# A hybrid decoder layer on one core: an attention weight load issued earlier, 1/rms multiplications paired, output weight pieces split later

## The chip, the cores and the metric

The kernel runs on one core of a Trainium2 chip. Its time is the device time of one execution, in microseconds (us). The engines are named as in the profile: PE (TensorE, matrix products; PEld is its loading of weights), DVE (VectorE), ACT (ScalarE), POOL (GpSimd) and SP (SyncE, which here issues nearly all DMAs). Each engine works through its own instructions in order; an instruction waits on semaphores for what other engines or DMAs have to finish first.

## The reference

One decoder layer for 256 tokens of width 1024, in float32. `h` is the RMS-normed input; `q`, `k`, `v`, `u_pool` and the gate logits are five parts of one projection of it.

```python
h = rmsnorm(x, norm_mix_g)
proj = h @ w_in
q, k, v, u_pool, gate_logits = split(proj)
q, k = rotary(rmsnorm(heads(q), q_norm_g)), rotary(rmsnorm(heads(k), k_norm_g))
attn = moba_attention(q, k, heads(v))       # 256 tokens are one block: causal attention
pooled = multiscale_pool_mixer(u_pool, w_pool, pool_scale)
gates = sigmoid(gate_logits + b_gate)       # two gates, one for each branch
mixed = gates[0] * (attn @ w_branch_attn) + gates[1] * (pooled @ w_branch_pool)
x = x + mixed @ w_out
h2 = rmsnorm(x, norm_ffn_g)
gate, val = split(causal_depthwise_conv(h2 @ w_up, conv_w, conv_b))
return x + (silu(gate) * val) @ w_down
```

## The kernel before

**Three products for one.** Every matrix product is made of three matmuls in a reduced float format (`mm3`, lines 101 to 107): each operand is split into a high part, which is the rounded value, and a low part, which is the rest. The product is high times high, plus high times low, plus low times high. So every weight passes through three steps: a DMA of a chunk of 128 x 2048 floats (1 MB) into one of four raw buffers; ACT writes its high part (`high`, line 93), DVE its low part (`low`, line 97). Both work on pieces of half a chunk, 128 x 1024.

**The schedule of the pieces.** `order` (line 110) lists the chunks as they are used: q, k, v, the pooled input `p`, the gates `g`, `pool`, two chunks `bp` of the pooled branch, two chunks `ba` of the attention branch, four chunks `o` of the output projection, then the feed-forward network. A call of `ahead()` (line 201) emits at most one high half and one low half, the next in the list; the low halves follow one piece behind the high ones. `next_high` does nothing when the chunk is four or more ahead of the oldest one still in use (`WBUFS`, line 169). After the last low half of a chunk its raw buffer is free, and `loads()` (line 191) emits the next load. Where `ahead()` is called, then, fixes on ACT, DVE and SP what stands in front of what: the order of every engine is the order in which the code emits.

**The stretch around the change.** After sixteen gate tiles (`g0` to `g15`) come eight tiles of the pooled branch (`bp`, j = 0 to 7, loop of line 739), then eight of the attention branch (`ba`, loop of line 763), then the output projection. A tile is 128 features for all 256 tokens: 12 matmul steps for a branch tile, 24 for an output tile. The tiles of PSUM rotate over four banks.

In a tile of the pooled branch DVE evicts PSUM and multiplies with the gate, which ACT has put through the sigmoid (line 671). Six gate tiles (`PLAIN`) were evicted by ACT without the 1/rms factor, and DVE multiplies each by `R1` later (line 757). Ahead of pooled tile 5, TensorE multiplies the softmax weights with the values (line 640); DVE scales the result by the reciprocal sums `RS` (line 659), ACT and DVE split it into the high and the low part of `heads` (lines 660 and 664).

In a tile of the attention branch there is a chain: DVE multiplies PSUM with the gate (line 770), POOL adds the pooled branch's tile (line 771), ACT writes the high part `mh[j]` (line 772), DVE the low part `ml[j]` (line 774), which for j - 2 is emitted at tile j. `mh` and `ml` are the moving operands of the output projection: its first output tile goes over k = 0 to 6, then the second over k = 0 to 6, then both over k = 7 (line 820).

**Softmax weights.** The weights of a pair of heads are turned by way of DRAM: a write (`home_w`, line 298) and four reads back, called fills (`sm<-home_w`, line 306). The sums of the exponentials are inverted, turned and written too (`home_sums`, lines 603 to 606); one tick later `fill_late` emits eight fills and asks for one load, and another tick later `spread` asks for one more and reads the sums back to all partitions (`RS`, line 628). From gate tile 10 on ordinary loads are paused, so that only these emit any.

Of the kernel before, what the change touches and what calls it, by code (L numbers as in the profile page):

```python
# [10 lines left out]
ALU = mybir.AluOpType  # L11
# [44 lines left out]
MAPS = 6  # L56
VALUES = 4
LATE = 9
PIECES = (1, 1, 1, 1, 0, 1, 1, 1)
GATES = (4, 5, 0, 1, 2, 6, 7, 3)  # L60
PLAIN = (4, 5, 6, 7, 8, 9)
HALVED = 2
# [10 lines left out]
def hybrid_layer_kernel(ctx: ExitStack, tc: tile.TileContext, xq_d, xtok_d, par_d, wkv_d, wpg_d,  # L73
                        wpool_d, wba_d, wbp_d, wout_d, wup_d, wdn_d, out_d):
    nc = tc.nc
# [16 lines left out]
    def high(hi, src, scale=1.0):  # L92
        nc.scalar.activation(hi, src, AF.Copy, scale=scale)  # L93

    def low(lo, hi, src, scale=None):
        if scale is None:
            nc.vector.tensor_tensor(lo, src, hi.bitcast(F32), ALU.subtract)  # L97
        else:
            nc.vector.scalar_tensor_tensor(lo, src, scale, hi.bitcast(F32), ALU.mult, ALU.subtract)
# [25 lines left out]
    def load(parts=1):  # L125
        c = loaded[0]
        if c == len(order):
            return
        loaded[0] += 1
        name, src = order[c]  # L130
        n = src.shape[-1]
        if c in cut_loads:
            parts = 2
        raws[c] = raw_p.tile([P, CH], F32, tag="raw", name=f"raw_{name}{c}")
        for i in range(parts):
            sl = slice(i * n // parts, (i + 1) * n // parts)
            nc.sync.dma_start(out=raws[c][:, sl], in_=src[:, sl])
# [53 lines left out]
    def loads(most=None):  # L191

        while loaded[0] - RAWBUFS in split and order[loaded[0] - RAWBUFS][0] != "q" and loaded[0] < len(order):
            if paused[0] if most is None else most == 0:
                break
            load()
            most = most if most is None else most - 1
# [3 lines left out]
    def ahead(upto=0):  # L201

        next_high()
        next_low()
        if at[1] - sum(p[0] < used[0] for p in pieces) < upto:
            next_high()
            next_low()

    def chunk(name):
        c = used[0]  # L210
        used[0] += 1
        spent.update(i for i in range(c) if order[i][0] != "dn")
        assert order[c][0] == name and all(p[0] != c or name == "dn" and p[3] for p in pieces[at[1]:]), (name, order[c][0])
        return his[c], los[c]
# [63 lines left out]
    R1 = const.tile([P, S], F32, name="R1")  # L278
# [12 lines left out]
    def turn(y, x):  # L291

        blocks = "p (n b r) -> p n b r"
        nc.vector.transpose(y.rearrange("p (b n r) -> p n b r", b=4, r=32), x.rearrange(blocks, b=4, r=32))

    def spill(y, name):
        home = dram.tile([P, y.shape[-1]], F32, name=f"home_{name}")
        nc.sync.dma_start(out=home, in_=y)
        return home
# [134 lines left out]
    def later(n, fn, *args):  # L434
        due.setdefault(clock[0] + n, []).append((fn, args))

    def tick():
        clock[0] += 1
        for fn, args in due.pop(clock[0], []):
            fn(*args)  # L440
# [80 lines left out]
    def gate(n):  # L521
        return gates[:, n // 2, n % 2, :]
# [58 lines left out]
    def exponentials(hp, sm, mx, *flat):  # L581
        for j in range(2):
            for t in (1, 0):
                at = j * H + NT * hp + t
                nc.scalar.activation(sm[:, j, TOK[t]], sm[:, j, TOK[t]], AF.Exp, bias=mx[:, t, j:j + 1],
                                     scale=qs[:, t, 2 * hp + j:2 * hp + j + 1], accum_out=rsum[:, at:at + 1])
        if hp % 2:
            later(1, held.append, (turn_weights, hp, *flat))
        else:
            later(2, turn_weights, hp, *flat)  # L590
# [4 lines left out]
    def turn_weights(hp, y, sm):  # L595
        turn(y, sm)
        home = spill(y, f"w{hp}")
        if hp < 2:
            later(1 + hp, fill_weights, hp, home, sm)
            return  # L600
        late.append((hp, home, sm))
        if hp == H // 2 - 1:
            nc.vector.reciprocal(rsum[:, 0:2 * H], rsum[:, 0:2 * H])
            yr = const.tile([P, 32], F32, name="yr")
            nc.vector.transpose(yr, rsum)
            far = spill(yr, "sums")
            later(1, fill_late, far)

    late = []
# [22 lines left out]
    def values(hps):  # L632

        po = ps2.tile([P, 2, 512], F32, tag="ps2", name=f"ps_o{hps[0]}")
        for i, hp in enumerate(hps):
            for b in range(2):
                for j in range(2):
                    h = 2 * hp + j
                    out = po[j * DH:(j + 1) * DH, i, 0:S].rearrange("p (a t r) -> p a t r", a=4, r=32)
                    nc.tensor.matmul(out[:, :, b:2, :], vn[:, b, h * DH:(h + 1) * DH],  # L640
                                     soft[hp][:, :, 3 * j + 2 * b:3 * j + b + 2, :], start=b == 0, stop=b == 1)
        return po
# [10 lines left out]
    def rounded(hps, po):  # L653
        if not heads:
            both = act.tile([P, 2, KA, S], F32R, tag="at", name="heads")
            heads.extend(both[:, i] for i in range(2))
        for i, hp in enumerate(hps):
            v = weighed(hp)
            nc.vector.tensor_tensor(v, po[:, i, 0:S].rearrange("p (a t r) -> p a t r", a=4, r=32), v, ALU.mult)
            high(tokens(heads[0], hp), natural(hp))  # L660

    def rests(hps):
        for hp in hps:
            low(tokens(heads[1], hp), tokens(heads[0], hp), natural(hp))
# [3 lines left out]
    def sigmoids(n):  # L668
        for _ in range(min(n, len(waiting))):
            f = waiting.pop(0)  # L670
            nc.scalar.activation(gate(f), gate(f), AF.Sigmoid, bias=par[:, C_BG + f:C_BG + f + 1])
# [19 lines left out]
    plain = []  # L691
    for n in range(2 * KD):
# [26 lines left out]
        f = 2 * GATES[b] + c  # L719
# [11 lines left out]
    def branch(src, oph, opl, j, w):  # L731
        hi, lo = w
        ps = bank(f"ps_b{src}{j}")
        for k in range(4):
            sl = slice(k * 512 + (j % 4) * P, k * 512 + (j % 4 + 1) * P)
            mm3(ps[:, 0:S], (hi[:, sl], lo[:, sl]), (oph[:, k, :], opl[:, k, :]), k == 0, k == 3)
        return ps

    for j in range(KD):
        if j % 4 == 0:  # L740
            w = chunk("bp")
        ps = branch("p", poolh, pooll, j, w)
        if j == VALUES:
            pos = [(hps, values(hps)) for hps in ((0, 1), (2, 3))]
        if j in (VALUES, VALUES + 1):
            nc.vector.tensor_tensor(gate(KD + j), ps[:, 0:S], gate(KD + j), ALU.mult)
            for hps, po in pos:
                rounded(hps, po) if j == VALUES else rests(hps)
        if j % 2 == 1:
            tick()  # L750
        for _ in range(PIECES[j]):
            ahead()
        sigmoids(1)
        if j not in (VALUES, VALUES + 1):
            nc.vector.tensor_tensor(gate(KD + j), ps[:, 0:S], gate(KD + j), ALU.mult)
        if j < len(plain):
            nc.vector.tensor_tensor(gate(plain[j]), gate(plain[j]), R1, ALU.mult)
    mixer.close()
    tmp = ctx.enter_context(tc.tile_pool(name="ffn", bufs=2))
    mh = act.tile([P, KD, S], F32R, tag="qk", name="mh")  # L760
# [2 lines left out]
    for j in range(KD):  # L763
        if j % 4 == 0:
            w = chunk("ba")
        ps = branch("a", heads[0], heads[1], j, w)
        sigmoids(1)
        if j in (1, 3):
            ahead()
        nc.vector.tensor_tensor(gate(j), ps[:, 0:S], gate(j), ALU.mult)  # L770
        nc.gpsimd.tensor_tensor(gate(j), gate(j), gate(KD + j), ALU.add)
        high(mh[:, j, :], gate(j))
        if j > 1:
            low(ml[:, j - 2, :], mh[:, j - 2, :], gate(j - 2))
# [248 lines left out]
```

## Time and profile before

| what | value |
| --- | --- |
| time, median of 3 runs | 329.81 us (329.2 to 329.86) |
| the profiled execution's own time | 328.35 us |
| its span in the trace | 326.5 us |
| busy: PE / DVE / ACT / POOL | 322.2 / 260.4 / 201.9 / 71.9 us |
| HBM read, written | 65.61 MB, 3.69 MB |

The span runs from the first to the last instruction in the trace; the profiled execution's own time has 1.85 us more around it. Busy time is the sum of an engine's instructions, without those that only wait, branch or issue DMAs. A row of a timeline has the start, the duration, the engine, the line, the operation and what it writes and reads; in square brackets stands how long the engine had been idle before it, and what ended that. Where rows are merged (x2 and more) the duration is that of all.

### The profile page before, as it was taken

How to read it: one execution, taken by the hardware profiler on the slowest of the kernel's cores; microseconds unless marked ns; L12 is line 12 of the kernel's file. 1: busy time of each engine (PE TensorE's matmuls, PEld its weight loads, DVE VectorE, ACT ScalarE, POOL GpSimd, SP SyncE). 2: the span in 40 equal slices, each digit the busy share in tenths (PEclk: the TensorE clock that was granted, in tenths of full speed). 3: DMA queues.
4: the chain of work that ended last, by engine and by line, in shares of the span. 5: the costliest groups of instructions: out<-in, count | busy, mean ns of one | idle time of the engine just before them, and what ended most of it. 6: DMA issues, size and time to landing. Idle time of an engine off the chain costs nothing.

```text
span 326.5 us, 6772 instructions
## 1 busy us (share of the span) xinstructions
PE 322.2 (99%) x2708; PEld 315.7 (97%) x2708; DVE 260.4 (80%) x451; ACT 201.9 (62%) x329; POOL 71.9 (22%) x89
## 2 busy tenths in 40 slices
PE   8999999999999999999999999999999999999995
PEld 8888899999999999999999999999999999999995
DVE  5839989999988986869997978686868686868834
ACT  5767619575968657668675647464646464646520
POOL 1007690000000070230421221212121212121330
PEclk9999999999999999999999999999999999999999
DMA  7999799838789743635437546464646464643003
GB/s 264 421 418 234 223 358 305 296 135 287 262 267 320 310 168 131 257 131 202 186 113 275 196 192 229 161 236 153 223 165 225 164 226 162 223 165 130 0 2 129
DMA packets 16542, 69.72 MB, mean 214 GB/s; under 512 B 2176, under 2 KB 7040, under 8 KB 9856
## 3 DMA queue, kind: packets, MB, share of 16 engines
q1 hardware_dynamic: 16096, 69.17, 59.8%
q8 instruction: 21, 0.34, 0.4%
q10 hardware_dynamic: 416, 0.13, 0.3%
q14 instruction: 9, 0.07, 0.1%
HBM read 65.61 MB, written 3.69 MB: 212 GB/s over the span
## 4 chain that ended last, share of the span: by engine, by line
PE 99%; DVE 0%; issue 0%
PE ps_up L106 12%; PE ps_up L105 12%; PE ps_up L107 12%; PE ps_d L884 6%; PE ps_d L883 6%; PE ps_d L885 6%; PE ps_g L105 4%; PE ps_g L106 4%; PE ps_g L107 4%; PE ps_q L335 3%; PE ps_k L335 3%; PE ps_v L335 3%; PE ps_out L106 2%; PE ps_out L107 2%; PE ps_out L105 2%; PE ps_warm L250 1%
## 5 line engine op out<-in xcount | busy, mean ns | idle before, releaser
L107 PE MATMUL ps_up<-hhi,lo_up 128*128 128x256 f32 x352 | 97.2, 276 | 0.0
L105 PE MATMUL ps_up<-hhi,hi_up 128*128 128x256 f32 x352 | 97.2, 276 | 0.0
L106 PE MATMUL ps_up<-hlo,hi_up 128*128 128x256 f32 x352 | 97.2, 276 | 0.0
L106 PEld LDWEIGHTS ps_up<-hlo,hi_up 128*128 128x128 f32 x352 | 66.1, 188 | 0.0
L105 PEld LDWEIGHTS ps_up<-hhi,hi_up 128*128 128x128 f32 x352 | 66.1, 188 | 0.0
L107 PEld LDWEIGHTS ps_up<-hhi,lo_up 128*128 128x128 f32 x352 | 66.1, 188 | 0.0
L97 DVE TENSOR_TENSOR lo_up<-raw_up,hi_up 128x1024 fp32r<-128x1024 f32 x44 | 54.7, 1262 | 7.3 <-ACT hi_up L93 7.3
L883 PE MATMUL ps_d<-ah,hi_dn 128*128 128x256 f32 x176 | 48.6, 276 | 0.0
L884 PE MATMUL ps_d<-al,hi_dn 128*128 128x256 f32 x176 | 48.6, 276 | 0.0
L885 PE MATMUL ps_d<-ah,lo_dn 128*128 128x256 f32 x176 | 48.6, 276 | 0.0
L93 ACT ACTIVATE hi_up<-raw_up 128x1024 fp32r<-128x1024 f32 x44 | 44.1, 1047 | 0.0
L865 POOL TENSOR_TENSOR c_v<-c_g,c_v 128x256 f32<-128x256 f32 x22 | 16.2, 738 | 121.4 <-DVE c_v L848 121.4
L93 ACT ACTIVATE ah<-c_v 128x256 fp32r<-128x256 f32 x22 | 9.2, 419 | 45.6 <-POOL c_v L865 45.6
L105 PE MATMUL ps_g<-xhi,hi_g 128*128 128x256 f32 x128 | 35.4, 277 | 0.0
L106 PE MATMUL ps_g<-xlo,hi_g 128*128 128x256 f32 x128 | 35.3, 276 | 0.0
L107 PE MATMUL ps_g<-xhi,lo_g 128*128 128x256 f32 x128 | 35.3, 276 | 0.0
L883 PEld LDWEIGHTS ps_d<-ah,hi_dn 128*128 128x128 f32 x176 | 33.0, 188 | 0.0
L884 PEld LDWEIGHTS ps_d<-al,hi_dn 128*128 128x128 f32 x176 | 33.0, 188 | 0.0
L885 PEld LDWEIGHTS ps_d<-ah,lo_dn 128*128 128x128 f32 x176 | 33.0, 188 | 0.0
L97 DVE TENSOR_TENSOR lo_dn<-raw_dn,hi_dn 128x1024 fp32r<-128x1024 f32 x22 | 27.8, 1264 | 0.4 <-ACT hi_dn L93 0.4
L853 DVE TENSOR_TENSOR u_v<-ps_up,R 128x256 f32<-128x256 f32 x22 | 9.3, 421 | 20.9 <-PE ps_up L107 20.8
L890 POOL TENSOR_TENSOR al<-c_v,ah 128x256 fp32r<-128x256 f32 x22 | 22.0, 1000 | 11.6 <-ACT ah L93 11.6
(189 smaller groups left out, 782.0 us busy)
## 6 DMA issues: line engine op xcount, KB each, us to landing
raw_up<-in_wup SPq DMA_DIRECT2D x22, 1024.0 KB, 4.9
raw_g<-in_wpg SPq DMA_DIRECT2D x8, 1024.0 KB, 8.5
raw_dn<-in_wdn SPq DMA_DIRECT2D x8, 1024.0 KB, 4.9
raw_o<-in_wout SPq DMA_DIRECT2D x4, 1024.0 KB, 10.1
raw_dn<-in_wdn SPq DMA_DIRECT2D x6, 512.0 KB, 4.9
raw_v<-in_wkv SPq DMA_DIRECT2D x2, 1024.0 KB, 15.3
raw_p<-in_wpg SPq DMA_DIRECT2D x2, 1024.0 KB, 12.7
raw_bp<-in_wbp SPq DMA_DIRECT2D x2, 1024.0 KB, 5.1
```

What stands on the lines that cost most here:

```text
L93: nc.scalar.activation(hi, src, AF.Copy, scale=scale)
L97: nc.vector.tensor_tensor(lo, src, hi.bitcast(F32), ALU.subtract)
L105: nc.tensor.matmul(out, sh, mh, start=start, stop=False, **kw)
L106: nc.tensor.matmul(out, sh, ml, start=False, stop=False, **kw)
L107: nc.tensor.matmul(out, sl, mh, start=False, stop=stop, **kw)
L335: nc.tensor.matmul(pt[t][:, c:c + wide], sx[:, k, t * P:(t + 1) * P], wx[:, sl], start=k == 0 and c == 0 and sx is xhi and wx is hi, stop= ...
L853: nc.vector.tensor_tensor(u, ps[:, 0:S], R2, ALU.mult)
L865: nc.gpsimd.tensor_tensor(uc[1], g[1], uc[1], ALU.mult)
L883: nc.tensor.matmul(o, hi[:, sl], acch[i], start=first, stop=False, skip_group_check=True)
L884: nc.tensor.matmul(o, hi[:, sl], accl[i], start=False, stop=False, skip_group_check=True)
L885: nc.tensor.matmul(o, lo[:, sl], acch[i], start=False, stop=i == KF - 1, skip_group_check=True)
L890: nc.gpsimd.tensor_tensor(accl[i], act_i, acch[i].bitcast(F32), ALU.subtract)
```

## The change

Three edits. The first emits one load directly behind the write of the reciprocal sums; the load that it emits is that of the first attention chunk `ba0`, which `fill_late` emitted before, behind the eight fills (its own call now finds no buffer free; the load of `ba1` stays with `spread`). The second multiplies two gates by `R1` at each of the pooled tiles 0, 1 and 2 instead of one at each of the tiles 0 to 5. The third takes away the calls of `ahead()` at the pooled tiles 5, 6 and 7 and has them in the attention branch at tiles 1, 2, 4 and 6 instead of 1 and 3.

```diff
-PIECES = (1, 1, 1, 1, 0, 1, 1, 1)
+PIECES = (1, 1, 1, 1, 0, 0, 0, 0)
...
             far = spill(yr, "sums")
+            loads(1)
             later(1, fill_late, far)
...
         if j not in (VALUES, VALUES + 1):
             nc.vector.tensor_tensor(gate(KD + j), ps[:, 0:S], gate(KD + j), ALU.mult)
-        if j < len(plain):
-            nc.vector.tensor_tensor(gate(plain[j]), gate(plain[j]), R1, ALU.mult)
+        for f in plain[2 * j:2 * j + 2]:
+            nc.vector.tensor_tensor(gate(f), gate(f), R1, ALU.mult)
...
         ps = branch("a", heads[0], heads[1], j, w)
         sigmoids(1)
-        if j in (1, 3):
+        if j in (1, 2, 4, 6):
             ahead()
         nc.vector.tensor_tensor(gate(j), ps[:, 0:S], gate(j), ALU.mult)
```

Followed through the lists of the code, the halves (0 and 1) that each call emits are these. Up to pooled tile 4 and from the call behind the attention branch on, both kernels emit the same.

| at tile | before: high (ACT), low (DVE) | with the change: high (ACT), low (DVE) |
| --- | --- | --- |
| pooled 5 | o0 half 0, ba1 half 1; load of o3 | none |
| pooled 6 | o0 half 1, o0 half 0 | none |
| pooled 7 | none (the chunk is four ahead) | no call |
| attention 1 | o1 half 0, o0 half 1; load of the first up chunk | o0 half 0, ba1 half 1; load of o3 |
| attention 2 | no call | o0 half 1, o0 half 0 |
| attention 3 | o1 half 1, o1 half 0 | no call |
| attention 4 | no call | o1 half 0, o0 half 1; load of the first up chunk |
| attention 6 | no call | o1 half 1, o1 half 0 |
| behind the branch | o2 half 0, o1 half 1 | o2 half 0, o1 half 1 |

In the attention branch the call stands ahead of the tile's eviction, so its low half is ahead of line 770 on DVE, and its high half is behind the preceding tile's `mh` on ACT.

## The prediction

> **What bounds the kernel now.** I read the page first, then the waits of PE, then the timeline around the attention branch.
>
> ```profile
> span 326.5 us, 6772 instructions
> PE 322.2 (99%) x2708; PEld 315.7 (97%) x2708; DVE 260.4 (80%) x451; ACT 201.9 (62%) x329; POOL 71.9 (22%) x89
> ...
> PEclk9999999999999999999999999999999999999999
> ```
>
> ```profile
> PE ps_warm L250 <- DVE ones L218: 1.1, 1, 1.1
> ```
>
> The second fence is the whole list of PE's waits: one, at the start. From 1.05 us on TensorE issues without a break at the full granted clock. No other engine has to become faster, so the change can gain next to nothing; it can only lose, by making TensorE wait. The question is how late each operand of TensorE may come, and what the change does to that. Next are TensorE's own dates, its first matmul of the attention branch and its first of the output projection:
>
> ```profile
> 110.61 0.28 PE L105 MATMUL ps_ba<-heads,hi_ba 128*128 128x256 f32 x1
> ...
> 121.48 0.28 PE L105 MATMUL ps_out<-mh,hi_o 128*128 128x256 f32 x1
> 121.60 0.28 PE L106 MATMUL ps_out<-ml,hi_o 128*128 128x256 f32 x1
> ```
>
> Eight tiles in 10.87 us: 1.36 us a tile. Tile j of the branch ends at about 112.14 + 1.36j (its last matmul starts 1.25 us after its first and takes 0.28). Output tile 0 goes over k = 0 to 6 in steps of three matmuls, 0.34 us, and its second matmul of step k reads ml[k]; so **ml[k] is due at 121.60 + 0.34k**: ml[4] at 122.95, ml[5] at 123.29, ml[6] at 123.63. (ml[7] comes after 14 steps, at 126.35.) Now VectorE, which makes them:
>
> ```profile
> 113.03 0.42 DVE L770 TENSOR_TENSOR xq<-ps_ba,xq 128x256 f32<-128x256 f32 x1
> 113.36 1.22 DVE L97 TENSOR_TENSOR lo_o<-raw_o,hi_o 128x1024 fp32r<-128x1024 f32 x1
> ...
> 115.67 0.50 DVE L97 TENSOR_TENSOR ml<-xq,mh 128x256 fp32r<-128x256 f32 x1 [0.36 <-ACT mh L93]
> ...
> 117.02 1.23 DVE L97 TENSOR_TENSOR lo_o<-raw_o,hi_o 128x1024 fp32r<-128x1024 f32 x1 [0.85 <-ACT hi_o L93]
> ...
> 122.64 0.68 DVE L97 TENSOR_TENSOR ml<-xq,mh 128x256 fp32r<-128x256 f32 x1 [0.20 <-ACT mh L93]
> ```
>
> The last row is ml[6]: done at 123.32, due at 123.63. **The slack is 0.3 us**, although the last low half of this stretch was over by 118.25. The change puts two more halves here, and the last of them ahead of the eviction of tile 6.
>
> **Prices**, from the groups of instructions between 96.9 and 125 us:
>
> ```profile
> L771 POOL TENSOR_TENSOR xq<-xq 128x256 f32<-128x256 f32 x8 | 7.6, 972 | 66.1 <-DVE xq L770 66.0
> L671 ACT ACTIVATE xq<-xq,par 128x256 f32<-128x256 f32 x13 | 6.1, 497 | 0.5 <-DVE xq L757 0.5
> L93 ACT ACTIVATE hi_o<-raw_o 128x1024 fp32r<-128x1024 f32 x5 | 5.2, 1049 | 0.0
> ...
> L97 DVE TENSOR_TENSOR lo_o<-raw_o,hi_o 128x1024 fp32r<-128x1024 f32 x4 | 4.9, 1220 | 0.9 <-ACT hi_o L93 0.9
> ...
> L770 DVE TENSOR_TENSOR xq<-ps_ba,xq 128x256 f32<-128x256 f32 x8 | 3.3, 418 | 0.1
> L93 ACT ACTIVATE mh<-xq 128x256 fp32r<-128x256 f32 x8 | 3.2, 415 | 5.8 <-POOL xq L771 5.8
> ...
> L757 DVE TENSOR_TENSOR xq<-xq,R 128x256 f32<-128x256 f32 x6 | 2.5, 416 | 0.0
> ```
>
> A low half is 1.22 us, a high half 1.05, an eviction 0.42, a high part mh 0.42, a low part ml 0.42 when alone. Rows that follow each other overlap by some 0.08 us on DVE (113.03 + 0.42 against 113.36) and 0.1 on ACT. The add on POOL has no one price:
>
> ```profile
> L771 POOL TENSOR_TENSOR xq<-xq x8: 737/917/1653, 113.5 to 122.2; 128x256 f32<-128x256 f32 x8
> ```
>
> ```profile
> 113.53 3.23 POOL L771 TENSOR_TENSOR xq<-xq 128x256 f32<-128x256 f32 x3 [64.14 <-DVE xq L770]
> ```
>
> ```profile
> 156.01 0.74 POOL L865 TENSOR_TENSOR c_v<-c_g,c_v 128x256 f32<-128x256 f32 x1 [10.50 <-DVE c_v L848]
> ```
>
> ```profile
> 156.12 1.71 DVE L97 TENSOR_TENSOR lo_up<-raw_up,hi_up 128x1024 fp32r<-128x1024 f32 x1
> ```
>
> The first add starts at 113.53, in the middle of the low half of 113.36 to 114.58, and takes 1.65 us instead of 0.74: it ends 0.6 us after the half does. The other way round, the half that starts 0.11 us into an operation of POOL takes 1.71 instead of 1.22, 0.49 more: POOL lets go 0.6 us after its start. So a low half and an add do not run together; who comes second waits. An eviction, which reads PSUM, stays at 0.42 beside them. With these prices I walked DVE, ACT and POOL through the branch of before; the walk gives each of their rows within 0.05 us (ml[6] at 122.65 to 123.31) and no wait of TensorE. The same walk is used below.
>
> **Part 1, the load of the first attention chunk.** It is one DMA of 1 MB, moved on SP past eight fills:
>
> ```profile
> 83.75 1.21 DVE L97 TENSOR_TENSOR lo_g<-raw_g,hi_g 128x1024 fp32r<-128x1024 f32 x1
> ```
>
> ```profile
> 86.31 0.55 SPq L298 DMA_DIRECT2D home_sums<-yr  x1
> 89.00 3.90 SPq L306 DMA_DIRECT2D sm<-home_w  x8
> 92.94 0.90 SPq L137 DMA_DIRECT2D raw_ba<-in_wba  x2
> 93.89 1.52 SPq L628 DMA_DIRECT2D RS<-home_sums  x2
> ```
>
> Its buffer is free by 84.96 (the low half of 83.75, the last of the chunk it replaces), so SP issues it at about 86.9, 0.4 us, inside the 2.1 us between 86.86 and 89.00 in which SP issues nothing today; the fills still start at 89.0 and everything behind them is issued 0.4 us sooner. In the rings the fills stand behind 1 MB.
>
> ```profile
> 87.00:88.00 1.00, 1.00 (x11) 1.00 (x10) 1.00 (x3) 1.00 (x2) 0.00 (x0) 1.00 1.03 404
> 88.00:89.00 1.00, 1.00 (x11) 1.00 (x11) 1.00 (x2) 1.00 (x3) 0.00 (x0) 1.00 0.28 83
> 89.00:90.00 1.00, 1.00 (x11) 1.00 (x11) 1.00 (x4) 0.48 (x1) 0.00 (x0) 1.00 0.05 13
> ```
>
> At 404 GB/s the megabyte takes 2.6 us, of which 1.7 fall into the empty stretch of 88 to 90; the fills land about 1 us later (bounds 0 and 2.6). Their reader, the values of TensorE below, starts at 103.66, ten us after the last fill is issued, so either bound costs nothing. The high half of this chunk waits for the load today, and DVE's low half for that:
>
> ```profile
> 103.66 2.82 PE L640 MATMUL ps_o<-sm,vn 128*64 128x256 f32 x32
> ```
>
> ```profile
> 98.01 1.06 ACT L93 ACTIVATE hi_ba<-raw_ba 128x1024 fp32r<-128x1024 f32 x1 [2.62 <-DMA raw_ba<-in_wba]
> ```
>
> ```profile
> 99.10 1.23 DVE L97 TENSOR_TENSOR lo_ba<-raw_ba,hi_ba 128x1024 fp32r<-128x1024 f32 x1 [1.71 <-ACT hi_ba L93]
> ...
> 104.87 0.42 DVE L755 TENSOR_TENSOR xq<-ps_bp,xq 128x256 f32<-128x256 f32 x1
> ...
> 105.87 1.42 DVE L659 TENSOR_TENSOR RS<-ps_o,RS 128x256 f32<-128x256 f32 x4
> ```
>
> That wait of ACT goes, and with it 1.7 us of idle DVE. TensorE reads the chunk first at 110.61, so the gain is no time.
>
> **Part 2, the multiplications by 1/rms.** Six of 0.42 us, none added; three come earlier. With the 1.7 us of part 1 DVE takes the eviction of pooled tile 3 at about 103.7 instead of 104.87 and reaches the values (row of 105.87) before TensorE has the second half of them, at 106.5; every gate is multiplied before its sigmoid. Cost nothing; the cover is DVE's wait for the values. Without part 1 the three extra ones would have been 1.2 us on DVE ahead of the heads, whose low parts, behind an eviction that TensorE releases at 108.1, have 1.9 us before the attention tiles.
>
> **Part 3, the pieces.** By the order of the code (the table ahead of this prediction) the attention branch has four calls in place of two, and before it two high and two low halves less are done. What this does, step by step (us):
>
> - DVE reaches tile 0 with nothing left over, at 112.17 in place of 113.03. Then the last low half of the second attention chunk, ahead of tile 1, runs 112.50 to 113.72. The first add starts at 112.67 inside it and ends at 114.31, mh[0] at 114.77.
> - ACT is in order: sigmoid, then the first high half of chunk o0, 115.08 to 116.13. Before, that half was done in the pooled branch.
> - DVE, at tile 2, has that low half next: it stands idle from 114.05 to 116.16, with the eviction of tile 2 (ready at 114.9) behind it. The half ends at 117.37, the eviction of tile 2 at 117.71, of tile 3 at 118.37.
> - The third low half is ready at 118.83 but meets the add of 118.60 to 119.52: 120.59. Tile 4 is evicted at 120.93; its add and mh[4], behind a high half, end at 122.31.
> - The fourth low half, ahead of tile 6, meets the add of tile 5: 122.06 to 123.83. Then come the eviction of tile 6 and ml[4], **done at 124.52, due at 122.95: 1.57 us**.
> - ml[5] behind the eviction of tile 7 is there at 125.40, due (shifted) at 124.86: 0.54. ACT has a high half between mh[5] and mh[6]; ml[6] comes at 126.28, due at 125.74: 0.54.
>
> **Sum**: 0 + 0 + 1.57 + 0.54 + 0.54 = **2.65 us**. TensorE has no slack anywhere to give it back. Behind the branch nothing else becomes late: the last low half of o1 ends at about 128.0, and TensorE reads it from step 4 of the second pair of tiles, 121.48 + 2.65 + 16 x 0.34 + 4 x 0.34 = 130.9; the loads of o3 and of the first up chunk, behind moved low halves on SP, go out at about 113.8 and 120.7, and ACT wants them only after an output tile, 126.2 + 2.65, against 10.1 and 4.9 us to land:
>
> ```profile
> raw_up<-in_wup SPq DMA_DIRECT2D x22, 1024.0 KB, 4.9
> ```
>
> ```profile
> raw_o<-in_wout SPq DMA_DIRECT2D x4, 1024.0 KB, 10.1
> ```
>
> Against its own time: 328.35 (span 326.5 and 1.85 around it) + 2.65 = 331.0. The runs' median, 329.81, lies 1.46 above the profiled execution; on it the forecast is **332.5**.
>
> How exactly the add and a half exclude each other is the disputed size. If they did not at all (every add 0.74, every half 1.22), the same walk gives ml[4], ml[5] and ml[6] with 0.86, 0.54 and 0.15 us to spare: a stall of 0. If POOL let go 0.4 us or 0.5 us after its start, 0.8 or 1.4. I take 0.6, since both rows above give it, and the walk of before fits.
>
> [...]
>
> **Rivals.**
> - *The pieces fit* (not slower): the attention branch starts 0.86 us earlier on DVE, and adds and halves fall beside each other. One mechanism, the order at each meeting of POOL and DVE; it decides from where ml[4] is done by 122.95. For it: 0.15 us of spare with no exclusion at all. Against: the 1653 ns row is just such a meeting, at the first add, where the change has a low half too. Time 329.8.
> - *Half of it*: POOL lets go sooner, or one of the two blocked low halves starts ahead of its add. Each such meeting is worth 0.55 us on the chain (118.83 to 119.38, 122.06 to 122.61): a stall of 0.7 to 2.1, at 1.4 a time of 331.2.
> - *Longer holds*: POOL keeps DVE out for its whole 0.74 us: up to 4.4 us, 334.2.
> - *A gain the profile does not show*: the timed runs are 1.46 us above the profiled one. Were that the values waiting for late sums:
>
> ```profile
> DMA to landing us min/median/max: 9.1/9.4/9.7
> ```
>
>   the sums, issued at 93.89 and 94.6, land by 104.3 and are first read at 105.87. 1.5 us of slack speaks against it; part 1 would give back at most 1.46: 328.35.
> - *The moved load hurts*: the fills or the sums late by more than their slack. The fills are issued by 92.9 and land 2.4 us later,
>
> ```profile
> sm<-home_w SPq DMA_DIRECT2D x16, 96.0 KB, 2.4
> ```
>
>   8 us ahead of the values; the sums have 1.5. The load takes 2.6: at most 1.1 us more, 333.6.
>
> **How the numbers follow.** Forecast (stall 2.2 to 3.2 us, its own range 332.0 to 333.0): 45%. Half of it: 20%. Longer holds: 8%. The moved load: 2%. The pieces fit: 18%. The hidden gain: 7%. This kernel's measurement tells 0.2%, 0.66 us, from no change. So slower 0.75, same 0.18, faster 0.07. The range 329.6 to 333.6 leaves out the gain and some of the fits below, and the longest holds above.
>
> **What would show it.** The changed profile should have waits of TensorE at L106, matmuls reading ml in the first output tile, for VectorE's L97, 2 to 3 us in all, the largest near 124; VectorE idle some 2 us near 115 for hi_o; ACT's wait for raw_ba gone; the fills landing before 100. I am wrong if PE's list of waits is still one row, or if the waits stand elsewhere: at L640 (part 1) or at the attention tiles.

## The result, and the profile after

The changed kernel takes 331.85 us (median of 9 executions, 330.85 to 333.29) and the kernel before, beside it on the same chip, 329.86 (328.79 to 330.55): 1.0069 times as long, 95% interval 1.0045 to 1.0092. The change makes the kernel slower by 2.0 us.

The page of the changed kernel, span, busy time and granted clock:

```profile
span 331.0 us, 6773 instructions
...
PE 324.7 (98%) x2708; PEld 317.2 (96%) x2708; DVE 261.6 (79%) x451; ACT 201.6 (61%) x329; POOL 72.1 (22%) x89
...
PEclk9999999999999997999999999999999999999999
```

The span is 4.5 us longer than the one the prediction is made against, and the sixteenth digit of the clock, 124 to 132 us, is a 7. The waits of TensorE (total us, times, longest):

```profile
PE ps_out L106 <- DVE ml L97: 1.9, 3, 1.4
PE ps_warm L250 <- DVE ones L218: 1.1, 1, 1.1
```

The new row stands where the prediction put it: in the first output tile, at the matmuls that read `ml`, for VectorE. The timeline of TensorE gives the three places, with the idle time in brackets:

```profile
124.64 0.39 PE L106 MATMUL ps_out<-ml,hi_o 128*128 128x256 f32 x1 [1.44 <-DVE ml L97]
...
125.52 0.39 PE L106 MATMUL ps_out<-ml,hi_o 128*128 128x256 f32 x1 [0.25 <-DVE ml L97]
...
126.39 0.39 PE L106 MATMUL ps_out<-ml,hi_o 128*128 128x256 f32 x1 [0.26 <-DVE ml L97]
```

Matmuls otherwise start every 0.11 us here. The starts of these three come 1.71, 0.54 and 0.53 us behind the matmul before, and the one behind each comes after 0.22 to 0.23 instead of 0.11. Beyond the usual pitch that is 1.60 + 0.43 + 0.42 + 0.33 = **2.78 us**; the 0.33 are the matmuls behind the three waits, called restarts below. The chain of waits shows what the time went through (start, length, instruction):

```profile
112.10 0.13 PE ps_ba L107
...
115.26 0.96 ACT hi_o L93
116.24 1.23 DVE lo_o L97
...
119.01 1.12 DVE lo_o L97
...
122.25 1.68 DVE lo_o L97
123.92 0.34 DVE xq L771
124.40 0.79 POOL xq L772
125.22 0.42 ACT mh L93
125.67 0.69 DVE ml L97
126.39 0.39 PE ps_out L106
```

It leaves TensorE at 112.23 and returns to it at 126.39, over the high half, the low halves, the evictions (`xq`, L771) and the adds of POOL that the prediction walked through. The two low halves that meet an add are the long ones; the group of low halves in this stretch (busy, mean ns):

```profile
L97 DVE TENSOR_TENSOR lo_o<-raw_o,hi_o 128x1024 fp32r<-128x1024 f32 x4 | 6.0, 1490 | 2.1 <-ACT hi_o L93 2.1
```

Their mean is 1490 ns where it was 1220.

These waits do not explain all of the 4.5 us. The same stretch in windows (PE, PEld, DVE, ACT and POOL busy, granted clock, DMA share, GB/s):

```profile
123.68:127.09 3.41, 1.94 (x12) 1.53 (x12) 3.01 (x8) 1.97 (x4) 1.66 (x2) 1.00 0.36 151
127.09:130.50 3.41, 3.41 (x19) 3.41 (x18) 1.01 (x1) 1.85 (x3) 0.00 (x0) 0.50 0.36 84
```

From 127.09 to 130.50 **TensorE has half its clock**; its matmuls start 0.21 us apart there instead of 0.11, and 3.41 us at half speed lose 1.7 us. 2.78 + 1.7 is the 4.5. Four of the nine executions have a mean granted clock of 0.995, this one among them (332.43 to 333.29), the other five 1.000 (330.85 to 331.85). The medians of the two groups, 332.9 and 331.1, are 1.8 us apart, about the price of one such stretch.

The third difference is at SP, where the load of `ba0` is issued at 87.41, as walked, but the rest is not earlier (start, length, issue):

```profile
86.86 0.42 SPq L298 DMA_DIRECT2D home_sums<-yr  x1
87.41 0.43 SPq L137 DMA_DIRECT2D raw_ba<-in_wba  x1
89.69 6.00 SPq L306 DMA_DIRECT2D sm<-home_w  x8
95.79 0.38 SPq L137 DMA_DIRECT2D raw_ba<-in_wba  x1
96.21 1.33 SPq L629 DMA_DIRECT2D RS<-home_sums  x2
```

```profile
SPq L306 <- DMA raw_ba<-in_wba: 2.2, 1, 2.2
```

The eight fills take 6.0 us to issue where they took 3.9: one of them waits 2.2 us until the megabyte has landed. So the load of `ba1` and the sums go out 2.3 us later than before, not 0.4 sooner, and ScalarE's wait has moved from the first half of `ba0` to the first of `ba1`:

```profile
95.83 1.05 ACT L93 ACTIVATE hi_ba<-raw_ba 128x1024 fp32r<-128x1024 f32 x1
...
101.38 1.06 ACT L93 ACTIVATE hi_ba<-raw_ba 128x1024 fp32r<-128x1024 f32 x1 [1.96 <-DMA raw_ba<-in_wba]
```

### The profile page after: what moved, and what is told of

Its sections match the earlier page's. It is cut to its first block, busy times and chain, and to the rows that moved or that the text cites. A ratio compares the mean times of both kernels' runs of the same rounds, so it can differ in the third digit from the quotient of the medians.

```text
span 331.0 us, 6773 instructions
## 1 busy us (share of the span) xinstructions
PE 324.7 (98%) x2708; PEld 317.2 (96%) x2708; DVE 261.6 (79%) x451; ACT 201.6 (61%) x329; POOL 72.1 (22%) x89
## 4 chain that ended last, share of the span: by engine, by line
PE 94%; DVE 3%; POOL 1%; ACT 1%; issue 0%; POOLq 0%
PE ps_up L106 12%; PE ps_up L107 12%; PE ps_up L105 12%; PE ps_d L885 6%; PE ps_d L886 6%; PE ps_d L884 6%; PE ps_g L105 4%; PE ps_g L106 4%; PE ps_g L107 4%; PE ps_q L335 3%; PE ps_k L335 3%; PE ps_v L335 3%; PE ps_out L106 2%; PE ps_out L107 2%; PE ps_out L105 2%; DVE lo_o L97 1%
```

## The experiments

Ratios are to the kernel before, run beside it on the same chip. Four questions: which part costs, which gains; whether the exclusion of POOL and VectorE makes the stall; whether each late half has the price of the walk; and where a gain can come from when TensorE has no wait.

### Parts 1 and 2 without part 3, and part 3 alone

The changed kernel with the pieces put back:

```diff
-PIECES = (1, 1, 1, 1, 0, 0, 0, 0)
+PIECES = (1, 1, 1, 1, 0, 1, 1, 1)
...
-        if j in (1, 2, 4, 6):
+        if j in (1, 3):
```

> Parts 1 and 2 of the change, with the pieces as before (load of the first attention chunk behind the sums' write, two multiplications a tile). If the pieces alone cost the time, TensorE waits nowhere behind its start: the ratio to before is 1.000 within its interval, granted clock 1.000. If the earlier load is a cause as well (in the changed profile the eighth fill, the second attention load and the sums go out 2.3 to 2.9 us later than before), TensorE or the last low parts come late and the ratio is above 1.002.

328.00 us, ratio **0.9952** (0.9933 to 0.9971). It is faster than both kernels. Its list of TensorE's waits is the one row of the warm-up at the start, as in the prediction's profile of before.

The kernel before with only part 3:

```diff
-PIECES = (1, 1, 1, 1, 0, 1, 1, 1)
+PIECES = (1, 1, 1, 1, 0, 0, 0, 0)
...
-        if j in (1, 3):
+        if j in (1, 2, 4, 6):
```

> Part 3 alone: the calls for pieces moved, the load and the multiplications as before. If the pieces alone cost the time: three waits of TensorE for ml[4], ml[5], ml[6], by the walk 1.57 + 0.54 + 0.54 = 2.65 us, as in the changed kernel, and the same ratio of about 1.007, with the clock halved for 3.4 us in some of the executions. If parts 1 and 2 took part, by making DVE reach the attention branch early, the waits differ by over 0.5 us.

332.56 us, ratio 1.0079 (1.0048 to 1.0110). Its waits:

```profile
PE ps_out L106 <- DVE ml L97: 1.9, 3, 1.4
...
PE ps_bp L105 <- DVE xq L755: 0.3, 1, 0.3
```

The row of the output tile is the same to the tenth, so part 3 alone makes the stall. The gain of the first two parts, 1.6 us by the ratio (1.8 between the medians), was not expected of a kernel without waits. The second row points to where it may come from: a wait for a bank of PSUM in the pooled branch, which the profile quoted in the prediction does not have.

### Does the exclusion of POOL and VectorE make the stall?

In the changed kernel POOL writes constants, for about as long, in place of adding the two branches, so the sum of the branches is left out of the result. POOL then reads no SBUF:

```diff
-        nc.gpsimd.tensor_tensor(gate(j), gate(j), gate(KD + j), ALU.add)
+        for n in (S, S, S // 2):
+            nc.gpsimd.memset(gate(j)[:, 0:n], 0.5)
```

> The changed kernel with POOL's add in the attention branch replaced by three writes of a constant into the same tile (of 256, 256 and 128 columns, together about as long as an add of 0.74 us). The sum of the two branches is left out. POOL then reads nothing there. If the add and the low halves exclude each other and this makes the stall, DVE's low halves take 1.22 us each, each group of writes 0.7 us or so, and by the walk without exclusion TensorE waits 0 us: ratio about 1.000. If the order of the queues alone makes it, waits of 1 us or more stay.

328.66 us, ratio 0.9979 (0.9958 to 1.0001). The low halves, and POOL's writes (duration min/median/max in ns):

```profile
L97 DVE TENSOR_TENSOR lo_o<-raw_o,hi_o x8: 1208/1218/1226, 116.4 to 134.7; 128x1024 fp32r<-128x1024 f32 x8
```

```profile
L773 POOL MEMSET xq<- x24: 205/312/316, 113.6 to 124.7; 128x256 f32 x16, 128x128 f32 x8
```

Every low half takes 1.21 to 1.23 us, although POOL is busy beside them for 0.83 us a tile. The list of TensorE's waits has no row for `ml`; one matmul reading `ml` starts 0.44 us behind its neighbour and the next 0.23, which is 0.45 us beyond the pitch in place of 2.78. (The list has one wait of 0.8 us, at the scores near 68 us, far ahead of the changed pieces.) So the same order of work costs little once POOL writes constants instead of reading two tiles from SBUF, and the halves beside it take 1.22 us instead of 1.75: the exclusion makes most of the stall.

### Does each late half have the price of the walk?

A second, identical low half behind that of tile 6, which prolongs the chain by one half:

```diff
             ahead()
+        if j == 6:
...
+            low(los[c][:, 0:CH // 2], his[c][:, 0:CH // 2], raw(c, slice(0, CH // 2)))
```

> The changed kernel with the low half ahead of attention tile 6 computed twice, 1.14 us more on DVE at the place named as the cause. By the walk the wait for ml[4] grows from 1.57 to 2.71 and the sum from 2.65 to 3.78 us. If the granted clock falls because TensorE idles too large a part of one stretch of 3.4 us (in the changed profile it was busy 1.94 of the 3.41 us ahead of the fall), the clock falls here in nearly every execution, for another 1.7 us: about 335. If it fell by chance, it falls in no more of the executions than in the changed kernel, 4 of 9.

334.05 us, ratio 1.0134 (1.0101 to 1.0167), with the wait for `ml`:

```profile
PE ps_out L106 <- DVE ml L97: 2.7, 1, 2.7
```

The matmul starts 2.97 us behind its neighbour, 2.86 beyond the pitch; the walk gives 2.71. The two waits behind it are gone from the list: from this one on the clock is at half for 6.83 us (125.50 to 132.33), TensorE's matmuls start 0.21 us apart instead of 0.11, and the operands that came late are now in time. The mean clock is 0.990 to 0.995 in all four executions.

The fourth call moved behind the branch, so that one half fewer stands on the chain:

```diff
-        if j in (1, 2, 4, 6):
+        if j in (1, 2, 4):
             ahead()
...
     ahead()
+    ahead()
```

> The changed kernel with the calls at attention tiles 1, 2 and 4 only and the fourth behind the branch, so that no low half stands ahead of the evictions of tiles 5 to 7. By the walk TensorE waits 0.10 us for ml[4], 0.54 for ml[5] and 0.54 for ml[6], 1.18 us in all instead of 2.65. Against parts 1 and 2 alone (0.995 of before) that is 0.4% more: a ratio of 0.998 to 1.000. No stretch of 3.4 us then has over 1.4 us of idle TensorE, so the granted clock stays 1.00 there in every execution. If the place of the fourth half does not matter, the ratio is that of the changed kernel, 1.007.

329.81 us, ratio 1.0003 (0.9976 to 1.0029).

```profile
PE ps_out L106 <- DVE ml L97: 0.5, 2, 0.3
```

Counted beyond the pitch, TensorE loses 1.30 us here, a quarter of it in restarts; the walk gives 1.18. The mean clock is 0.998 to 1.000 in all twelve executions; in the profiled one, at 0.998, it falls only in the last 1.2 us of the span. Parts 1 and 2 gain about as much, 1.6 us, and so the kernel is as fast as before.

The four calls kept, but each behind the tile's `mh` and `ml` instead of ahead of its eviction:

```diff
-        if j in (1, 2, 4, 6):
-            ahead()
         nc.vector.tensor_tensor(gate(j), ps[:, 0:S], gate(j), ALU.mult)
...
+        if j in (1, 2, 4, 6):
+            ahead()
```

> The changed kernel with the four calls behind the tile's eviction, mh and ml instead of ahead of the eviction. By the walk this only shifts the wait by a tile: 0.19 us for ml[4], 2.01 for ml[5], 0.54 for ml[6], 2.73 us in all, and the clock falls in some executions: a ratio of 1.005 to 1.010. If standing ahead of the eviction is what costs the time, the waits shrink to below 1 us and the ratio to 0.998 or less.

332.98 us, ratio 1.0093 (1.0058 to 1.0128).

```profile
PE ps_out L106 <- DVE ml L97: 1.7, 1, 1.7
```

The three matmuls start 0.32, 2.00 and 0.53 us behind their neighbours, which is 0.21, 1.89 and 0.42 beyond the pitch; the walk's stalls are 0.19, 2.01 and 0.54. The halves only make another `ml` the late one: their being there so late, not their place in the tile, makes the stall. The mean clock is 0.994 or 0.995 in eight of ten executions.

### Where does the gain come from?

Part 1 alone (one added `loads(1)` behind the spill of the sums), and part 2 alone (the loop over two gates in place of one):

> Part 1 alone: the load of the first attention chunk behind the sums' write. Parts 1 and 2 together took 0.48% off. Theory: in most executions of the kernel before, unlike its profiled one, that load lands so late that DVE evicts the pooled tiles late and TensorE waits for a free bank of PSUM; the earlier load removes it, so this kernel has the whole gain, a ratio of about 0.995. Rival: the gain is that of the multiplications, then the ratio is 1.000 here.

> Part 2 alone: two multiplications a tile at the pooled tiles 0 to 2. By the theory that the late load is the cause, three more multiplications, 1.2 us, stand on DVE between the late low halves and the evictions: a ratio of 1.000 to 1.004, not below. By the rival it has the gain, about 0.995.

Part 1 alone: 328.41 us, ratio 0.9960 (0.9939 to 0.9981). Part 2 alone: 328.94 us, ratio 0.9980 (0.9966 to 0.9995). The gain of the pair, 0.9952, is mostly part 1's. That part 2 gains 0.2% by itself was a miss: it was to stay at 1.000.

The kernel before itself once more, for a second profile of it:

> The kernel before once more, for a second profile of it. The first profiled execution, 328.35 us, was among its fastest; the middle of its executions is near 329.8. If the late load is the cause of that, an execution near the middle has ACT waiting for raw_ba more than the 2.62 us of the first profile, and waits of TensorE at the pooled tiles of 1 us or more; if it is something else, the same waits as in the first profile and the time elsewhere.

This execution took 329.95 us, the one behind the prediction 328.35. Its waits, beside the one at the start:

```profile
PE ps_ba L105 <- DVE xq L755: 0.5, 1, 0.5
PE ps_bp L105 <- DVE xq L755: 0.4, 1, 0.4
```

**So the kernel before does make TensorE wait; the one profile did not show it.** With their restarts the two rows are 1.4 us beyond the pitch, of the 1.6 us between the two executions. The timeline of the same profile shows the first of them in order of time, that of `ps_bp` (SP, ScalarE, VectorE, TensorE):

```profile
90.24 3.91 SPq L306 DMA_DIRECT2D sm<-home_w  x8
94.20 0.91 SPq L137 DMA_DIRECT2D raw_ba<-in_wba  x2
```

```profile
99.86 1.06 ACT L93 ACTIVATE hi_ba<-raw_ba 128x1024 fp32r<-128x1024 f32 x1 [4.54 <-DMA raw_ba<-in_wba]
```

```profile
100.95 1.23 DVE L97 TENSOR_TENSOR lo_ba<-raw_ba,hi_ba 128x1024 fp32r<-128x1024 f32 x1 [3.63 <-ACT hi_ba L93]
102.10 0.42 DVE L755 TENSOR_TENSOR xq<-ps_bp,xq 128x256 f32<-128x256 f32 x1
```

```profile
102.66 0.36 PE L105 MATMUL ps_bp<-poolh,hi_bp 128*128 128x256 f32 x1 [0.36 <-DVE xq L755]
```

The fills start at 90.24 instead of 89.00, so the load of `ba0` is issued at 94.20 instead of 92.94, and its first high half runs at 99.86 instead of 98.01. VectorE's low half of it stands ahead of the eviction of pooled tile 0, the bank that tile 4 needs is not free, and TensorE waits. In the prediction's profile the same eviction is over at 100.66, 1.5 us before the same matmul:

```profile
100.24 0.42 DVE L755 TENSOR_TENSOR xq<-ps_bp,xq 128x256 f32<-128x256 f32 x1
```

```profile
102.20 0.28 PE L105 MATMUL ps_bp<-poolh,hi_bp 128*128 128x256 f32 x1
```

The second wait, at 114.60, belongs to the same lateness: VectorE works without a break from the first low half of `ba1`, at 105.38, to the evictions at 114.12 (112.37 in the prediction's profile), the first of which releases it; the high half ahead of that low half had waited 0.82 us for the load of `ba1`.

If that is the mechanism, a still later load must cost more. The kernel before without the `loads(1)` in `fill_late` and in `spread`, so that both loads go out behind the reads of the sums:

```diff
             fill_weights(*weights)
-        loads(1)
         later(1, spread, far)
...
     def spread(far):
 
-        loads(1)
         RS.append(big("RS"))
```

> The kernel before with the loads of both attention chunks emitted behind the read of the sums, some 1.5 us later on SP and behind 0.5 MB more. If a late load makes TensorE wait, its list of waits has rows at the pooled tiles (L105, for DVE's evictions) or at the heads, 1 to 3 us in all, ACT waits over 4 us for the load, and the ratio is 1.003 to 1.01. If not, the ratio is 1.000.

335.21 us, ratio 1.0146 (1.0114 to 1.0179), 4.8 us by the ratio and more than was expected; the mean clock is 0.990 to 0.994 in all four executions, which is part of it.

```profile
PE ps_bp L105 <- DVE xq L753: 4.7, 1, 4.7
```

```profile
104.60 1.06 ACT L93 ACTIVATE hi_ba<-raw_ba 128x1024 fp32r<-128x1024 f32 x1 [8.88 <-DMA raw_ba<-in_wba]
```

The same kind of wait at the same matmul, the first of pooled tile 4, over ten times as long. Both directions agree on the gain's source: later `ba` loads (both moved here) lengthen the wait for a bank of the pooled branch, an earlier `ba0` (the first experiment) takes it away. The profiles agree too: the six of kernels with parts 1 and 2 have no wait for an eviction at the matmuls of the two branches; of the five in which `ba0` is loaded as before or later, four have one, all but the one behind the prediction. The spread of the times says it too: the kernel with parts 1 and 2 lies between 327.88 and 328.89 us, the kernel before beside it between 327.89 and 331.59, with one more at 333.40 whose mean clock was 0.995. The fastest executions are alike; what goes is the upper end.

How part 2 gains was not tried by itself. Its three early multiplications leave VectorE's queue between the late evictions, and its profile has no wait at the first attention tiles where the second profile of before has 0.5 us, though it keeps one of 0.4 us in the pooled branch; that fits, but one profile of each is no proof, since this wait varies.

## Why the prediction was right, and where it was not

The time, 331.85 us, is 0.65 below the 332.5 forecast and inside the range of 329.6 to 333.6, just short of the forecast's own range of 332.0 to 333.0. The cause was the right one. That the number came so close is in part luck: the sum lacks a gain of 1.6 us and a loss of 0.8 us to the clock, of opposite sign.

- **Part 3, the chain: right, step by step.** VectorE idle for `hi_o`: 2.10 us, up to 116.24 (forecast 114.05 to 116.16). Third low half: over at 120.70 (120.59), fourth at 123.92 (123.83). `ml[4]` done at 124.59 (124.52). Stalls of 1.60, 0.43 and 0.42 (1.57, 0.54, 0.54) and 0.33 of restarts, which had no term of their own: 2.78 against 2.65.
- **The exclusion: right, and its size too.** The two blocked halves take 1.76 and 1.75 us, the first add 1655 ns. "Half of it" and "longer holds" are both out: the stall is 2.78 us, no run shows the 4.4 of the second, and POOL lets go before its add is over. The rows of VectorE and of POOL (two adds each):

```profile
118.94 1.76 DVE L97 TENSOR_TENSOR lo_o<-raw_o,hi_o 128x1024 fp32r<-128x1024 f32 x1
...
122.17 1.75 DVE L97 TENSOR_TENSOR lo_o<-raw_o,hi_o 128x1024 fp32r<-128x1024 f32 x1
```

```profile
117.88 1.74 POOL L772 TENSOR_TENSOR xq<-xq 128x256 f32<-128x256 f32 x2 [2.78 <-DVE xq L771]
121.17 1.68 POOL L772 TENSOR_TENSOR xq<-xq 128x256 f32<-128x256 f32 x2 [1.55 <-ACT hi_o L93]
```

  The halves end at 120.70 and 123.92; 1.22 earlier is 119.48 and 122.70, and the adds end at 119.62 and 122.85, 0.14 and 0.15 later.

  Beside POOL's writes of constants a half takes 1.21 to 1.23 us. How long an add keeps a half out is measured here: all of the add but its last 0.14 to 0.15 us, if the half then takes its usual 1.22.
- **"From 1.05 us on TensorE issues without a break ... so the change can gain next to nothing": wrong.** This is the step that failed. It was true of the profiled execution, one of the fastest, and not of the kernel. The rival "a gain the profile does not show" (7%) had the right clue, the 1.46 us between the profile and the median, but put it down to late sums; it was the load of the attention chunks. For that load the prediction asked when TensorE reads the chunk, at 110.61, and not what stands behind its low half on VectorE: the eviction of pooled tile 0, with 1.5 us of slack in the profile and none in the second one. Parts 1 and 2 gain 0.48%, 1.6 us, close to the 1.46 that the rival allowed.
- **Parts 1 and 2, "gain no time": wrong for the same reason.** Setting the forecast on the median, 329.81 + 2.65, then counted the 1.46 of old waits as if they would stay.
- **"Everything behind them is issued 0.4 us sooner": wrong by 2.7 us.** In the changed kernel the eighth fill waits 2.2 us for the load, and the eight land 5.2 us behind their issue (median) where they took 2.4. So ScalarE's wait for `raw_ba`, which was to be gone, moved to `ba1` (1.96 us). It made no wait of TensorE in the profile of the changed kernel. It can: part 1's own slowest execution has the first half of `ba1` at 105.27, behind a 5.98 us wait, and then TensorE waits 0.3 us in the pooled branch and 0.5 and 1.1 us at the attention tiles. This is what part 1 still leaves open.
- **The clock: not foreseen.** No term of the sum; 1.7 us in four of nine executions, 0.8 in the mean.

Put together on the means of the executions, since 0.8 is a mean (the median execution, 331.85, has a clock of 1.000): 328.16 for the kernel with parts 1 and 2, + 2.78 + 0.8 = 331.7, of 331.96 measured. Against before: -1.6 for the waits that go, +2.8 for those that come, +0.8 for the clock, 2.0 us slower.

## What to carry to other kernels

One profile is one execution: where it lies at the fast end of the runs, the waits that make up the median may be missing from it, so profile again before calling an engine free of waits. Count the slack of each operand as a date, and that of the work queued behind its pieces as well. Keep pieces of VectorE work out of a chain that alternates between VectorE and GpSimd adds (here a low half of 1.22 us took 1.75 beside an add); the late load was cured here by issuing it earlier, and parts 1 and 2 without part 3 are the version to keep (0.9952). Here waits of TensorE cost more than their length: in five profiles a stretch of 3.41 us with 1.4 us or more of them stood ahead of at least 3.41 us at half the clock, which lose 1.7 us; behind one with 1.1 us the clock stayed full (last section).

## What was not expected of the hardware

**The clock fell behind stretches in which TensorE was busy for up to 59% of the time.** The falls last 3.41 us (changed kernel, part 3 alone, calls behind the eviction) or 6.83. In each of the five profiles with a fall inside the work it starts a whole number of stretches of 3.413 us (29, 35 or 36) behind the point, 4.21 to 6.78 us into the span, at which the trace's record of the clock begins and the matmuls get faster: in the changed kernel 15 of them lie in the 3.41 us before 4.21 and 27 in those after, and 127.09 is 4.21 + 36 x 3.413. The 3.41 us ahead of a fall are called its window here. TensorE's busy time in it, the second figure, was 1.94 in the changed kernel, quoted above, 1.65 with the calls behind the eviction, and with part 3 alone

```profile
123.96:127.37 3.41, 2.02 (x12) 1.61 (x13) 3.01 (x8) 1.97 (x4) 1.66 (x2) 1.00 0.30 127
```

Where there is no fall, windows can be placed by the same count of stretches; that the count holds there too is an estimate from the five falls. Of these, that of the kernel with three calls has 2.91 (121.94 to 125.35), and the least busy one is in the profile of part 1 alone, at its waits of the attention tiles:

```profile
114.00:117.41 3.41, 2.34 (x21) 2.14 (x20) 3.41 (x7) 1.00 (x3) 1.14 (x1) 1.00 0.79 250
```

So TensorE was busy for 2.02 us or less in the windows with a fall behind them, which is 1.4 us or more of waits, and for 2.34 us or more in these without one, 1.1 us of waits or less. All of them are at full clock; at half clock one with 2.99 us busy, in the profile of the extra low half, was followed by another at half. In the changed kernel TensorE was busy for 57% of the window, and the longest distance between two matmul starts around it was 1.71 us. Why only some executions fall was not shown: no execution of the changed kernel without a fall was profiled.

**A DMA issued on SP waited for one issued eight DMAs earlier to land**: 2.2 us of SP, with all behind it in the queue. In the changed kernel it is the eighth fill, issued at 95.39; the load of 87.41 landed 8.0 us behind its issue. All seven profiles with the earlier load have such a wait, of 0.8 to 2.8 us. What makes it wait was not shown.

**The same load took very different times to land.** From its issue to landing, the median of the two `ba` loads was 6.1 us in the profile behind the prediction, 7.5 in the second profile of before and 8.7 in that of part 1 alone; the single loads of the two profiles of before took 5.0 to 9.5. The 1.5 us of slack that pooled tile 0 had in the first of them was gone in the second.
